# One plain chunk per feed-forward block instead of two, two chunks opened with plain gate blocks, operand sums in another order

## The chip, the cores and the metric

One NeuronCore of one Trainium2 chip runs the whole program. The time is device microseconds (us) from the first to the last instruction of one execution, as the runs report it; lower is better. The engines are named as in the profile: PE (matrix products), PEld (its weight loads), DVE (vector), ACT (scalar/activation), POOL (GpSimd) and SP (the queue that issues most loads from memory).

## What is computed

Two layers of a hybrid encoder over 512 + 256 = 768 tokens of width 1024. Each layer is feed-forward, mixer, feed-forward, with residuals; the first mixer is a gated linear recurrence (HGRN2), the second a windowed attention. The change touches only the four feed-forward blocks:

```python
def swiglu_ffn(x, w1, w2):
    gate, up = jnp.split(x @ w1, 2, axis=-1)
    return (jax.nn.silu(gate) * up) @ w2
...
x = x + 0.5 * swiglu_ffn(rmsnorm(x, norm_g[li, 0]), ffn_w1[li, 0], ffn_w2[li, 0])
```

w1 is 1024 x 5632 (gate columns, then up columns), w2 is 2816 x 1024, everything float32.

## The kernel before

**Products in three passes.** Every float32 operand is split into a high part (`hi`, a cast on ACT) and the rest (`lo`, a subtraction on DVE); a product is hi·hi + hi·lo + lo·hi. So each weight costs an ACT cast and a DVE subtraction before PE can use it: lines 166 and 167 for a plain weight of 128x1024, lines 199 and 200 for the pieces of the scheme below (there one piece in seven, p5, has its subtraction on POOL).

**Chunks and groups.** The 2816 hidden columns are NF = 22 chunks of 128. The first two of a block (PLAIN = 2) are computed plainly: gate and up, two halves of 384 tokens, 8 x 3 products each, 96 matmuls a chunk in all. Every other chunk ("quad", `up_pair`) uses a Winograd-Strassen scheme: the gate tile and the up tile, cut at half the depth, give a11, a12 (gate) and a21, a22 (up), and seven products p1 to p7 of 12 matmuls replace eight, 84 matmuls a chunk. Their order on PE is UP: p1, p7, p2, p5, p4, p6, p3. The p5 and p3 products go into the same PSUM bank `d`; between them, line 446 (`w = w - d`) has to read the bank. After every four chunks a "down" quad multiplies with w2 by the same scheme on 512-wide tiles (order DOWN: p1, p2, p5, p4, p7, p6, p3; 18 matmuls each, 126 in all), and line 506 adds each result to the residual `x`. There are five such groups in a block, so 20 in the program, then two chunks and a plain last product.

**Weights on their way.** `plan_ffn` writes a queue of loads. `load_next` takes its head and issues the loads into raw buffers `wr`: there are four (RAWBUFS), a quad of up chunks takes two (gate tile, up tile), a down quad four, a plain weight one. Two loads that add, both issued by POOL (line 141), form `s3 += a11` (for p7) and `a21 += a22`. Two DVE additions in place (line 206) follow: "second" a11 += a21, and "fourth" a12 += a11; p6 and p3 are split from their results. A raw buffer is free again when its last piece is split: the up tile after p4 and p5, the gate tile after p3.

**What sets the order.** A list scheduler puts each engine's instructions in order; it may move an instruction forward from its place in the program text when its operands and buffers are free. Split weights lie in eight `w` tiles (WBUFS). `held` counts them: a staged piece adds 1 or 2, `release` takes that off again, and `ahead`, called after nearly every product, stages further pieces as long as `held` stays within eight. `take` stages a piece at its use if `ahead` has not done so before. The second and fourth additions are pinned: `keep_in_program_order` makes such an instruction follow the instruction that was written just before it for the same engine. So the place at which a step is written matters for those two, and for the casts that wait for them.

Of the kernel before, what the change touches and what calls it, by code (L numbers as in the profile page):

```python
# [12 lines left out]
AF = mybir.ActivationFunctionType  # L13
# [32 lines left out]


class Trunk:
# [123 lines left out]
    def quad_steps(self, key, raws, srcs, order):  # L172
# [204 lines left out]
    def plan_ffn(self, tag, w1, w2):  # L377
        def up(i):
            gate, up = (w1[:, c * P : (c + 1) * P] for c in (i, NF + i))
            if i < PLAIN:  # L380
                self.plan((tag, i, 0), gate, (NC, P))
                self.plan((tag, i, 1), up, (NC, P))
            else:
                self.plan_quad((tag, i), (gate, up), (NC, P), UP)

        for g in range(GROUPS):
            for i in range(4 * g, 4 * g + 4):
                up(i)
            rows = w2[4 * g * P : (4 * g + 4) * P, :].rearrange("(a k p) c -> k p a c", p=P, k=2)
            srcs = [rows[k][:, :, c * 512 : (c + 1) * 512] for c in range(2) for k in range(2)]  # L390
            self.plan_quad((tag, "down", g), srcs, (2, 512), DOWN)
        for i in range(NF - 2, NF):
            up(i)
        for c in range(2):
            self.plan((tag, "last", c), w2[(NF - 2) * P :, c * 512 : (c + 1) * 512], (2, 512))

    def up_plain(self, tag, j, half):
        pss = []
        for c in range(2):
            wh, wl = self.take((tag, j, c))  # L400
            ps = self.ps(H)
            for k in range(NC):
                b = self.operand(f"b{k // 4}{half}", k % 4)
                self.mm3(ps, (wh[:, k, :], wl[:, k, :]), b, k == 0, k == NC - 1)
                if half == 0 and k in (((), (2, 6)), ((3, 7), (3, 7)))[j][c]:
# [6 lines left out]
        self.nc.vector.tensor_mul(t, t, pss[1])  # L412
        return t

    def product(self, key, name, src, ps, first, last):
        wh, wl = self.take((*key, name))
        for k in range(4):
            a, b = (wh[:, k, :], wl[:, k, :]), self.operand(src, k)
            for i, (x, y) in enumerate(((0, 0), (0, 1), (1, 0))):
                self.nc.tensor.matmul(  # L420
                    ps,
# [3 lines left out]
                    stop=k == 3 and i == 2,  # L425
                    skip_group_check=True,
                )
        self.release((*key, name))

    def up_pair(self, tag, j):  # L430
        nc = self.nc
        key = (tag, j)
        a, b, c, d = (self.ps(H) for _ in range(4))
        v, w, t = (self.tmp(H) for _ in range(3))
        p = lambda name, ps, first, last: self.product(key, name, FACTOR[name], ps, first, last)
        p("p1", a, True, False)
        nc.scalar.copy(v, a)
        self.ahead()
        p("p7", c, True, False)
        nc.scalar.copy(w, c)  # L440
        self.ahead()
        p("p2", a, False, True)
        nc.scalar.activation(a, a, AF.Silu)
        self.ahead()
        p("p5", d, True, False)
        nc.vector.tensor_sub(w, w, d)
        self.ahead()
        p("p4", c, False, True)
        p("p6", b, True, True)
        nc.vector.tensor_sub(v, v, b)  # L450
        nc.vector.tensor_sub(t, c, v)
        nc.vector.tensor_mul(t, t, a)
# [55 lines left out]
    def ffn(self, tag, next_row):  # L508
        for g in range(GROUPS):
            hid = {}  # L510

            def put(name, src, kp):
                if name not in hid:
                    hid[name] = self.big([P, 2, 2, H], F32R)
                self.split(src, hid[name][:, kp, 0, :], hid[name][:, kp, 1, :])

            def gather(ts, kp):
                self.mix(ts[0], ts[1], ts[2], ts[3], lambda name, src: put(name, src, kp))

            if g == 0:  # L520
                ts = {}
                for half in range(2):
                    for j in range(PLAIN):
                        t = ts[2 * j + half] = self.up_plain(tag, j, half)
                        name = f"b{j}{half}"
                        if name != "b01":
                            put(name, t, 0)
                gather(ts, 0)
                self.run_later(len(self.deferred))
            for kp in range(2):  # L530
                if g == 0 and kp == 0:
                    continue
                ts = []
                for j in range(2):
                    for half, t in enumerate(self.up_pair(tag, 4 * g + 2 * kp + j)):
# [753 lines left out]
```

## Time and profile before

| | |
|---|---|
| median of 3 runs | 2816.7 us (2816.09 to 2816.84) |
| the profiled execution: its time | 2815.21 us |
| its span from first to last instruction | 2813.4 us |
| granted PE clock, mean over the span | 0.998 |
| ACT busy | 1324.6 us, 47% of the span |
| POOL busy | 366.5 us, 13% |
| read from memory | 216.39 MB |

The page of the profile is one execution. The row of an engine gives its busy time; in the rows by line, "out<-in xcount | busy, mean ns" are a group of equal instructions, and what stands behind the second bar is how long their engine sat idle before them and what ended that. PE's instructions overlap, so busy time divided by count (not the mean of one) is the pace at which they follow each other.

### The profile page before, as it was taken

The numbers are of one execution on the slowest core, as the hardware profiler recorded it, in microseconds if no ns is written. First come the engines' busy times: TensorE is split into PE (matmuls) and PEld (weight loads), VectorE is DVE, ScalarE is ACT, GpSimd is POOL, SyncE is SP. The second block draws the span as 40 slices with busy tenths as digits, with TensorE's granted clock in tenths as the row PEclk, the third lists the DMA queues.
The fourth block names the chain that finished last, engine by engine and source line by source line (L and its number), as shares of the span: only waits on it lengthen the run. The fifth ranks groups of instructions, "written<-read, shape, count | busy, mean of one in ns | idle before, by whom it ended". The sixth has DMA issues, their size and how long they took to land.

```text
span 2813.4 us, 40558 instructions
## 1 busy us (share of the span) xinstructions
PE 2781.1 (99%) x15225; PEld 2557.6 (91%) x15225; DVE 2162.5 (77%) x3750; ACT 1324.6 (47%) x2453; POOL 366.5 (13%) x402
## 2 busy tenths in 40 slices
PE   8999999999999999999999999999999999999998
PEld 8999999889899889999999999999988789999998
DVE  7788788478577558878878887887858878878877
ACT  7444443434344336444444644444457756444443
POOL 1111121000000001111111111111103211211111
PEclk9999999999999999999999999999999999999999
DMA  6554554311111133555454255545422113655543
GB/s 165 133 126 114 124 142 121 112 46 38 39 45 38 60 97 76 135 131 124 114 127 127 75 136 133 129 112 129 135 72 76 32 52 83 143 135 124 120 114 108
DMA packets 330102, 291.37 MB, mean 104 GB/s; under 512 B 11609, under 2 KB 257841, under 8 KB 329905
## 3 DMA queue, kind: packets, MB, share of 16 engines
q1 hardware_dynamic: 294064, 212.43, 25.8%
q0 software_dynamic: 31680, 62.93, 13.0%
q10 hardware_dynamic: 4160, 13.42, 1.4%
q8 instruction: 119, 1.95, 0.3%
q14 instruction: 79, 0.64, 0.1%
HBM read 216.39 MB, written 9.44 MB: 80 GB/s over the span
## 4 chain that ended last, share of the span: by engine, by line
PE 95%; ACT 2%; DVE 2%; POOL 0%; issue 0%; DMA 0%; DVEq 0%; SPq 0%; ACTq 0%; POOLq 0%
PE ps L420 41%; PE ps L484 20%; PE ps L262 8%; PE ps L261 8%; PE ps L260 8%; PE ps L676 3%; PE ps L770 1%; PE ps L322 1%; PE ps L746 1%; PE ps L1151 1%; ACT big L1129 0%; PE ps L1113 0%; PE ps L1164 0%; PE ps L1114 0%; PE ps L915 0%; PE ps L1163 0%
## 5 line engine op out<-in xcount | busy, mean ns | idle before, releaser
L420 PE MATMUL ps<-big,w 128*128 128x384 f32 x6720 | 1169.2, 334 | 0.0
L420 PEld LDWEIGHTS ps<-big,w 128*128 128x128 f32 x6720 | 1165.9, 188 | 1.6
L199 ACT CAST w<-wr 128x512 fp32r<-128x512 f32 x600 | 416.2, 707 | 684.3 <-PE ps L420 277.6
L484 PE MATMUL ps<-w,big 128*128 128x512 f32 x2520 | 575.3, 389 | 0.0
L484 PEld LDWEIGHTS ps<-w,big 128*128 128x128 f32 x2520 | 472.7, 188 | 97.5
L200 DVE TENSOR_TENSOR w<-wr,w 128x512 fp32r<-128x512 f32 (+1 forms) x520 | 433.5, 837 | 152.8 <-ACT w L199 132.0
L506 DVE SCALAR_TENSOR_TENSOR x<-ps,x 128x512 f32<-128x512 f32 x468 | 301.9, 683 | 10.0 <-PE ps L262 10.0
L141 POOL DMA_DIRECT2D s<-wr x120 | 105.0, 875 | 1536.5 <-DMA wr<-in_ffn_w_dram 632.7
L260 PE MATMUL ps<-w,big 128*128 128x512 f32 x624 | 249.4, 400 | 0.3
L262 PE MATMUL ps<-w,big 128*128 128x512 f32 x624 | 244.7, 392 | 2.1 <-DVE big L989 1.1
L261 PE MATMUL ps<-w,big 128*128 128x512 f32 x624 | 244.0, 391 | 0.0
L260 PE MATMUL ps<-big,w 128*128 128x384 f32 (+2 forms) x640 | 220.8, 346 | 3.4 <-ACT big L265 2.0
L261 PE MATMUL ps<-big,w 128*128 128x384 f32 (+2 forms) x640 | 217.0, 339 | 0.6 <-DVE big L266 0.4
L262 PE MATMUL ps<-big,w 128*128 128x384 f32 (+2 forms) x640 | 215.7, 337 | 0.0
L265 ACT CAST big<-tA 128x384 fp32r<-128x384 f32 x296 | 148.0, 513 | 114.8 <-DVE tA L459 36.2
L167 DVE TENSOR_TENSOR w<-wr,w 128x1024 fp32r<-128x1024 f32 x92 | 111.9, 1222 | 83.6 <-ACT w L166 78.2
L266 DVE TENSOR_TENSOR big<-tA,big 128x384 fp32r<-128x384 f32 x296 | 166.0, 571 | 6.7 <-ACT big L265 4.4
L200 POOL TENSOR_TENSOR w<-wr,w 128x512 fp32r<-128x512 f32 x80 | 131.4, 1643 | 195.5 <-ACT w L199 195.5
L166 ACT CAST w<-wr 128x1024 fp32r<-128x1024 f32 x92 | 96.6, 1052 | 121.5 <-PE ps L261 100.7
L262 PEld LDWEIGHTS ps<-w,big 128*128 128x128 f32 x624 | 117.2, 188 | 28.3 <-DVE big L989 2.0
L141 POOL DMA_DIRECT2D wr<-wr x100 | 87.3, 873 | 403.1 <-DMA wr<-in_ffn_w_dram 165.6
L206 DVE TENSOR_TENSOR wr<-wr,wr 128x512 f32<-128x512 f32 (+1 forms) x120 | 125.3, 1044 | 17.8 <-issue 15.9
(169 smaller groups left out, 3273.6 us busy)
## 6 DMA issues: line engine op xcount, KB each, us to landing
wr<-in_ffn_w_dram SPq DMA_DIRECT2D x264, 512.0 KB, 4.0
s<-in_ffn_w_dram SPq DMA_DIRECT2D x120, 256.0 KB, 3.2
s<-wr POOLq DMA_DIRECT2D x120, 256.0 KB, 4.8
wr<-wr POOLq DMA_DIRECT2D x80, 256.0 KB, 3.8
wr<-in_hg_w_in_dram SPq DMA_DIRECT2D x40, 512.0 KB, 3.8
wr<-wr POOLq DMA_DIRECT2D x20, 512.0 KB, 4.6
spill<-x ACTq DMA_DIRECT2D x12, 512.0 KB, 2.9
x<-spill ACTq DMA_DIRECT2D x12, 512.0 KB, 3.3
```

The lines of the kernel that those rows point to most:

```text
L141: self.nc.gpsimd.dma_start(out, src, accum_op=ALU.add)
L199: nc.scalar.copy(h, src)
L200: (eng or nc.vector).tensor_sub(l, src, h.bitcast(F32))
L206: add = {"second": lambda: nc.vector.tensor_add(a11, a11, a21), "fourth": lambda: nc.vector.tensor_add(a12, a12, a11)}
L260: nc.tensor.matmul(out, a[0], b[0], start=first, stop=False)
L261: nc.tensor.matmul(out, a[0], b[1], start=False, stop=False)
L262: nc.tensor.matmul(out, a[1], b[0], start=False, stop=last)
L265: self.nc.scalar.copy(hi, src)
L266: self.nc.vector.tensor_sub(lo, src, hi.bitcast(F32))
L420: self.nc.tensor.matmul(ps, a[x], b[y], start=first and k == 0 and i == 0, stop=k == 3 and i == 2, skip_group_check=True,)
L484: nc.tensor.matmul(ps, a[x], w[y], start=name == chain and kp == 0 and q == 0, stop=kp == 1 and q == 2, skip_group_check=True,)
L506: self.nc.vector.scalar_tensor_tensor(x, ps, c, x, ALU.mult, ALU.add)
```

## The change

PLAIN becomes 1. Chunks 1 and 2 of a block (OPENED) have their gate computed by `open_pairs` from a plain gate weight, on the first 384 tokens, before the operands of the second half exist; their remaining five products follow as REST: p5, p7, p6, p4, p3. For them the subtraction of p5 goes to DVE. `sums`, which forms the operands t1 to t4 of a block, forms them in the order t1, t3, t2, t4 for both halves of the depth, where it formed all four for one half and then for the other. In `plan_ffn` the plain gate weights of both opened chunks are planned in the branch that every quad chunk takes.

```diff
-PLAIN = 2
+PLAIN = 1
+OPENED = range(PLAIN, PLAIN + 2)
...
+REST = ("p5", "p7", "p6", "p4", "p3")
...
-            split(name, own[name], nc.gpsimd if up and name == "p5" else None)
+            split(name, own[name], nc.gpsimd if order == UP and name == "p5" else None)
...
     def sums(self):
-        for kp in range(2):
-            tiles = (self.tn[(i // 2, i % 2)][:, kp] for i in range(4))
-            self.mix(*tiles, lambda name, src: self.put(name, kp, src))
+        sub = self.nc.vector.tensor_sub
+        quads = [[self.tn[(i // 2, i % 2)][:, kp] for i in range(4)] for kp in range(2)]
+        for kp, (b11, b12, b21, b22) in enumerate(quads):
+            sub(b22, b12, b22)
+            sub(b12, b11, b12)
+            self.put("t1", kp, b12)
+        for kp, (b11, b12, b21, b22) in enumerate(quads):
+            self.put("t3", kp, b22)
+        for kp, (b11, b12, b21, b22) in enumerate(quads):
+            sub(b11, b11, b22)
+            self.put("t2", kp, b11)
+        for kp, (b11, b12, b21, b22) in enumerate(quads):
+            sub(b21, b21, b11)
+            self.put("t4", kp, b21)
...
             else:
-                self.plan_quad((tag, i), (gate, up), (NC, P), UP)
+                for j in OPENED:
+                    self.plan((tag, j, "gate"), w1[:, j * P : (j + 1) * P], (NC, P))
+                self.plan_quad((tag, i), (gate, up), (NC, P), REST if i in OPENED else UP)
...
+    def open_pairs(self, tag, js):
+        opened = {j: (self.ps(H), self.tmp(H)) for j in js}
+        for part in range(2):
+            for j, (a, v) in opened.items():
+                key = (tag, j, "gate")
+                w = tuple(t[:, 4 * part : 4 * part + 4, :] for t in self.take(key))
+                self.multiply(a, w, FACTOR["p2" if part else "p1"], not part)
+                if part:
+                    self.nc.scalar.activation(a, a, AF.Silu)
+                    self.done(key)
+                else:
+                    self.nc.scalar.copy(v, a)
+                self.run_later()
+        return opened
...
-    def up_pair(self, tag, j):
+    def up_pair(self, tag, j, opened=None):
...
+        if opened:
+            p("p5", d, True, False)
+            self.ahead()
+            p("p7", c, True, False)
+            nc.scalar.copy(w, c)
+            nc.vector.tensor_sub(w, w, d)
+            self.ahead()
+            p("p6", b, True, True)
+            p("p4", c, False, True)
+        else:
...
             if g == 0:
-                ts = {}
-                for half in range(2):
-                    for j in range(PLAIN):
-                        t = ts[2 * j + half] = self.up_plain(tag, j, half)
...
+                plain = [self.up_plain(tag, 0, 0)]
+                put("b00", plain[0], 0)
+                opened = self.open_pairs(tag, OPENED)
                 self.run_later(len(self.deferred))
+                plain.append(self.up_plain(tag, 0, 1))
```

Three places show what stands in a row now. The line numbers of the changed kernel are a little higher: 549 is the old 506 (adding to x), 208 the old 206 (second and fourth), 202 the old 200 and 169 the old 167 (subtractions of a split), 489 the old 446, 493 the old 450.

**The queue of loads (SP), second group of the first block.** `wr_257` and `wr_258` are the gate and up tile of one chunk, `wr_260` and `wr_261` of the next, and so on; `s3` is the extra tile for p7. Before:

```order
L151 DMA wr_258_1735<-in_ffn_w1_dram 128x8x128
L151 DMA wr_260_1741<-in_ffn_w1_dram 128x8x128
L151 DMA wr_261_1743<-in_ffn_w1_dram 128x8x128
L185 DMA s3_278_1866<-in_ffn_w1_dram 128x4x128
L151 DMA wr_276_1862<-in_ffn_w1_dram 128x8x128
L151 DMA wr_277_1864<-in_ffn_w1_dram 128x8x128
```

Now:

```order
L153 DMA wr_332_2047<-in_ffn_w1_dram 128x8x128
L153 DMA wr_333_2049<-in_ffn_w1_dram 128x8x128
L153 DMA wr_344_2081<-in_ffn_w1_dram 128x8x128
L153 DMA wr_347_2087<-in_ffn_w1_dram 128x8x128
L187 DMA s3_386_2365<-in_ffn_w1_dram 128x4x128
L153 DMA wr_356_2195<-in_ffn_w1_dram 128x8x128
L153 DMA wr_357_2197<-in_ffn_w1_dram 128x8x128
L153 DMA wr_373_2248<-in_ffn_w1_dram 128x8x128
L153 DMA wr_376_2254<-in_ffn_w1_dram 128x8x128
```

Between the tiles of one chunk (332, 333) and of the next (356, 357) two further loads of the same size stand now (344, 347; then 373, 376): the plain gate weights of chunks 1 and 2 once more.

**The down quad on DVE, second half of it.** `x` rows add a product's results (three rows a product, one for each block of tokens); `wr_331`/`wr_405` is a11 of this down quad. Before, with `ps_359` to `361` holding p7 and the `x_5` to `x_7` rows ahead of it the end of p4:

```order
L506 SCALAR_TENSOR_TENSOR x_7_98<-ps_354_2445,x_7_98 128x512
L206 TENSOR_TENSOR wr_331_2265<-wr_331_2265,wr_333_2269 128x1024
L506 SCALAR_TENSOR_TENSOR x_10_104<-ps_359_2485,x_10_104 128x512
L506 SCALAR_TENSOR_TENSOR x_11_106<-ps_360_2493,x_11_106 128x512
L200 TENSOR_TENSOR w_358_2482<-wr_331_2265,w_357_2481 128x1024
L506 SCALAR_TENSOR_TENSOR x_12_108<-ps_361_2501,x_12_108 128x512
L206 TENSOR_TENSOR wr_332_2267<-wr_332_2267,wr_331_2265 128x1024
```

Now, with p7 in `ps_427` to `429` and p6 in `ps_432` to `434`:

```order
L549 SCALAR_TENSOR_TENSOR x_12_108<-ps_429_2676,x_12_108 128x512
L208 TENSOR_TENSOR wr_405_2504<-wr_405_2504,wr_407_2508 128x1024
L202 TENSOR_TENSOR w_431_2686<-wr_405_2504,w_430_2685 128x1024
L549 SCALAR_TENSOR_TENSOR x_10_104<-ps_432_2689,x_10_104 128x512
L549 SCALAR_TENSOR_TENSOR x_11_106<-ps_433_2697,x_11_106 128x512
L549 SCALAR_TENSOR_TENSOR x_12_108<-ps_434_2705,x_12_108 128x512
L208 TENSOR_TENSOR wr_406_2506<-wr_406_2506,wr_405_2504 128x1024
L202 TENSOR_TENSOR w_436_2715<-wr_406_2506,w_435_2714 128x1024
L169 TENSOR_TENSOR w_450_2759<-wr_437_2718,w_449_2758 128x1024
L169 TENSOR_TENSOR w_453_2765<-wr_438_2720,w_452_2764 128x1024
```

The second addition (208, first row of that line) stood ahead of all three additions of p7's result and stands now behind the last of them; the fourth stands behind the last addition of p6's result, and the split of p3 behind that.

**An up chunk on DVE.** `wr_332` belongs to chunk B, the second of its group, `wr_356` to chunk C, the third; line 489 is B's reading of the bank `d`. Now:

```order
L202 TENSOR_TENSOR w_355_2192<-wr_332_2047,w_355_2192 128x512
L169 TENSOR_TENSOR w_372_2245<-wr_344_2081,w_371_2244 128x1024
L169 TENSOR_TENSOR w_375_2251<-wr_347_2087,w_374_2250 128x1024
L202 TENSOR_TENSOR w_377_2256<-wr_356_2195,w_377_2256 128x512
L202 TENSOR_TENSOR w_378_2272<-s3_358_2199,w_378_2272 128x512
L202 TENSOR_TENSOR w_379_2288<-wr_356_2195,w_379_2288 128x512
L489 TENSOR_TENSOR tA_340_2075<-tA_340_2075,ps_339_2074 128x384
L208 TENSOR_TENSOR wr_356_2195<-wr_356_2195,wr_357_2197 128x512
```

Behind the split of B's p3 stand the splits of two repeated gate weights (169), then C's p1, p7 and p2, and only then B's line 489.

More of the change, by code (lines that the diff above doesn't have):

```diff
@@ L404, in up_plain @@
                 self.mm3(ps, (wh[:, k, :], wl[:, k, :]), b, k == 0, k == NC - 1)
-                if half == 0 and k in (((), (2, 6)), ((3, 7), (3, 7)))[j][c]:
+                if half == 0 and k in ((), (2, 6))[c]:
                     self.run_later()
@@ L413, in up_plain, with product, multiply @@
         return t
-    def product(self, key, name, src, ps, first, last):
-        wh, wl = self.take((*key, name))
+    def product(self, key, name, src, ps, first):
+        self.multiply(ps, self.take((*key, name)), src, first)
+        self.release((*key, name))
+    def multiply(self, ps, w, src, first):
         for k in range(4):
-            a, b = (wh[:, k, :], wl[:, k, :]), self.operand(src, k)
+            a, b = (w[0][:, k, :], w[1][:, k, :]), self.operand(src, k)
             for i, (x, y) in enumerate(((0, 0), (0, 1), (1, 0))):
@@ L431, in up_pair @@
+    def up_pair(self, tag, j, opened=None):
         nc = self.nc
         key = (tag, j)
[L433 to L449, printed above, removed]
+        a, v = opened or (self.ps(H), self.tmp(H))
+        b, c, d = (self.ps(H) for _ in range(3))
+        w, t = (self.tmp(H) for _ in range(2))
+        p = lambda name, ps, first, last: self.product(key, name, FACTOR[name], ps, first)
+        if opened:
[8 more added lines that the diff above has]
+        else:
+            p("p1", a, True, False)
+            nc.scalar.copy(v, a)
+            self.ahead()
+            p("p7", c, True, False)
+            nc.scalar.copy(w, c)
+            self.ahead()
+            p("p2", a, False, True)
+            nc.scalar.activation(a, a, AF.Silu)
+            self.ahead()
+            p("p5", d, True, False)
+            nc.vector.tensor_sub(w, w, d)
+            self.ahead()
+            p("p4", c, False, True)
+            p("p6", b, True, True)
```

14 lines of the change are left out of this document (6 added, 8 removed).

## The prediction

> **What bounds the kernel now.** I read the page first: busy shares, then the chain of work that ended last, then the costliest groups.
>
> ```profile
> span 2813.4 us, 40558 instructions
> ...
> PE 2781.1 (99%) x15225; PEld 2557.6 (91%) x15225; DVE 2162.5 (77%) x3750; ACT 1324.6 (47%) x2453; POOL 366.5 (13%) x402
> ...
> PE 95%; ACT 2%; DVE 2%; POOL 0%; issue 0%; DMA 0%; DVEq 0%; SPq 0%; ACTq 0%; POOLq 0%
> ...
> L420 PE MATMUL ps<-big,w 128*128 128x384 f32 x6720 | 1169.2, 334 | 0.0
> ...
> L484 PE MATMUL ps<-w,big 128*128 128x512 f32 x2520 | 575.3, 389 | 0.0
> ```
>
> PE is busy 99% of the span and carries 95% of the chain: its pace is the time. An up matmul takes 1169.2/6720 = 0.174 us, a down matmul 575.3/2520 = 0.228 us. So a product of an up chunk is 12 x 0.174 = 2.09 us, a chunk 14.6 us, a down quad 28.7 us. The waits of PE, longest first and the last, say how little is left to gain:
>
> ```profile
> PE ps L111 <- DMA tB<-in_hg_g_norm_dram: 7.5, 1, 7.5
> PE ps L915 <- DVE big L266: 3.1, 3, 1.9
> ...
> PE ps L261 <- DVE big L266: 0.4, 1, 0.4
> ```
>
> There are eleven such rows, 23 us together, none at an up or down product. A change can gain only by giving PE fewer instructions; it can lose wherever it uncovers a wait. The cover, in one down quad and the four chunks behind it:
>
> ```profile
> 257.50:286.00 28.50, 28.50 (x127) 23.59 (x126) 28.09 (x46) 10.19 (x17) 4.92 (x5) 1.00 0.58 136
> 286.00:344.50 58.50, 58.50 (x338) 58.46 (x338) 41.62 (x69) 27.54 (x49) 10.08 (x10) 1.00 0.51 123
> ```
>
> Columns after the length: PE, PEld, DVE, ACT, POOL busy, PE clock, share of the transfer engines, GB/s. DVE has almost no slack in a down quad and 17 us in four chunks.
>
> **The change part by part.** *Removed:* one plain chunk a block. 96 matmuls become 84, 48 fewer over four blocks: 48 x 0.174 = 8.4 us off PE, the whole of the possible gain.
>
> *Added:* the planning line stands in the branch of every quad chunk. So both plain gate weights are queued ahead of each of 21 quads: 42 a block, 168 in all, where 8 are used. What the 160 repeats cost, by a plain weight's split:
>
> ```profile
> L167 DVE TENSOR_TENSOR w<-wr,w 128x1024 fp32r<-128x1024 f32 x92 | 111.9, 1222 | 83.6 <-ACT w L166 78.2 <-PE ps L420 4.7
> ...
> L166 ACT CAST w<-wr 128x1024 fp32r<-128x1024 f32 x92 | 96.6, 1052 | 121.5 <-PE ps L261 100.7 <-PE ps L420 20.1 <-DVE w L167 0.3
> ...
> q1 hardware_dynamic: 294064, 212.43, 25.8%
> ...
> wr<-in_ffn_w_dram SPq DMA_DIRECT2D x264, 512.0 KB, 4.0
> ...
> s<-wr POOLq DMA_DIRECT2D x120, 256.0 KB, 4.8
> wr<-wr POOLq DMA_DIRECT2D x80, 256.0 KB, 3.8
> wr<-wr POOLq DMA_DIRECT2D x20, 512.0 KB, 4.6
> ```
>
> ACT gets 168 us more and DVE 196, spread over the span; four chunks bring DVE eight repeats, 9.8 us, to 51.4 of 58.5 us. The 84 MB more are 102 us of transfer time (3.4 us a MB by q1's row). All that fits beside PE: no engine becomes the bound by its sum, and I cost it at nothing. Two other things are not free. The repeats hold two of the four raw buffers, so a chunk's tiles load only when the chunk before has left its own. And `held` grows by 4 with every quad and is never taken down (a repeat overwrites its staged entry, and is released once at most). After the third quad it stays at eight or more, `ahead` returns at once, and each piece is staged where it is used. Casts and splits still move forward; the pinned additions don't. So now the walk, with one group's order.
>
> *Pinned additions (40 places).* In the profile the second and fourth additions and their splits stand far ahead of use:
>
> ```profile
> 257.45 28.76 PE L484 MATMUL ps<-w,big 128*128 128x512 f32 x126
> ...
> 269.28 1.22 DVE L206 TENSOR_TENSOR wr<-wr,wr 128x1024 f32<-128x1024 f32 x1
> ...
> 271.67 1.23 DVE L200 TENSOR_TENSOR w<-wr,w 128x1024 fp32r<-128x1024 f32 x1
> ...
> 276.24 1.23 DVE L200 TENSOR_TENSOR w<-wr,w 128x1024 fp32r<-128x1024 f32 x1 [0.41 <-ACT w L199]
> ...
> 270.58 1.06 ACT L199 CAST w<-wr 128x1024 fp32r<-128x1024 f32 x1 [4.61 <-DVE wr L206]
> ...
> L506 DVE SCALAR_TENSOR_TENSOR x<-ps,x 128x512 f32<-128x512 f32 x468 | 301.9, 683 | 10.0 <-PE ps L262 10.0
> ```
>
> p6 starts 5 x 4.1 us after 257.45, at 278.0; its split ends at 272.9. Now, after p7's last matmul: addition to x 0.68, second addition 1.22, cast 1.06, and PE may start p6; three matmuls (0.68) run with the high part while the subtraction takes 1.23. Idle: 0.68 + 1.22 + 1.06 + (1.23 - 0.68) = 3.5, and 0.3 for five hand-overs (the cast above starts 0.08 after its addition): 3.8 us. p3 waits likewise behind p6. Two places, 20 quads: 40 x 3.8 = **152 us**. Bounds 140 (no hand-overs) and 200 (DVE still has queued work ahead).
>
> *First chunk after a down quad (20).* The small pieces cost:
>
> ```profile
> L199 ACT CAST w<-wr 128x512 fp32r<-128x512 f32 x480 | 291.6, 620 | 413.3 <-PE ps L420 212.3 <-PE ps L484 64.7 <-DVE wr L206 57.3
> ...
> L200 DVE TENSOR_TENSOR w<-s,w 128x512 fp32r<-128x512 f32 x120 | 82.5, 687 | 17.4 <-ACT w L199 17.1
> ...
> L450 DVE TENSOR_TENSOR tA<-tA,ps 128x384 f32<-128x384 f32 x80 | 44.1, 551 | 41.5 <-PE ps L420 41.2
> ...
> 285.78 1.88 DVE L506 SCALAR_TENSOR_TENSOR x<-ps,x 128x512 f32<-128x512 f32 x3
> ```
>
> DVE instructions that follow each other overlap a little: three of 0.68 take 1.88, a pace of 0.60. Let p6 end at 0. The addition to x and the fourth addition end at 2.0 and free the raw buffer of the next gate tile, whose load lands 4.0 later with its issue, at 6.2. Meanwhile the cast and split of p3 end at 4.4; PE, which has three matmuls of p3 behind it, needs 15 x 0.228 = 3.4 more and comes to the new chunk at 7.8. On DVE two repeats (to 6.8) and two additions to x (8.0) stand ahead of its p1 split, which ends at 8.6; PE has two matmuls of high parts to do (0.35) and then waits 0.45. p1 ends at 10.3. The s3 transfer, issued at 6.2, lands at 11.0; cast and split end at 12.4, where PE could have gone on at 10.65: 1.75 lost. **20 x 2.2 = 44 us**; 0 if loads land earlier, 80 if each stands behind one repeat (512 KB, 1.8 us by q1's row).
>
> *Inside a group (20).* PE adds p3(B) into bank `d` only when B's line 489 has read it, and line 489 stands behind C's p7 split. On the same clock A ends on PE at 24.7, and p3(B) is due six products later, at 37.2. The split of p3(A) ends at 16 (its cast stands behind the copy that waits for p7(A), 14.4) and frees the buffer for B's up tile. That lands at 20.0 and is added into by 24.5, with issue; B's p7 and p2 splits, the second addition and line 493 bring the split of p4(B) to 27.2. This frees the buffer for C's gate tile: landed 31.2, s3 36.0, cast and split 37.3, p2 37.9, line 489 38.4. **20 x 1.2 = 24 us**; 0 to 60, since one transfer that is 2 us late comes through in full. C and D have line 489 ahead of the next p7 and just make it.
>
> *Into the down quad (20).* D starts at 55.1 by the same walk; its p3 split, behind C's last vector steps and two repeats, ends at 61.3. The fourth raw tile of the down quad loads only then (65.4) and is added into the third (70.0); cast and split of the down quad's p5 end near 72.4, and D's last six steps (0.47 to 0.60 apart), which stand behind that split, bring b10's low part near 76.4. PE, done with D at 69.8, wants it for p2 at 69.8 + 4.1 + 1.1 = 75.0. **20 x 1.5 = 30 us**; 0 to 70.
>
> *A block's start (4).* Chunks 1 and 2 give PE 60 matmuls, 10.4 us, but the loop of their up tile (4.0 + 3.8, then two additions and splits of p4, p6, p3 at 0.6 to 0.7 with casts between) is about 14: 2 x 3.6 = 7; **28 us**, 0 to 60. The new order of `sums` and the p5 subtraction on DVE lie under the plain second half (48 matmuls, 8.4 us): t1 needs six steps of 0.95 at most, 5.7 us; bare, that would cost 23 in all. Mixers: their casts carry no pin and stand where they stood; 0.
>
> ```profile
> L266 DVE TENSOR_TENSOR big<-big,big 128x768 fp32r<-128x768 f32 x64 | 58.2, 952 | 11.5 <-ACT big L265 11.5
> ```
>
> *The clock.* One pause of PE inside the program shows it:
>
> ```profile
> 26.00:28.00 2.00, 0.72 (x4) 0.33 (x3) 1.58 (x4) 1.99 (x4) 0.54 (x1) 1.00 0.58 101
> 576.00:578.00 2.00, 0.96 (x6) 0.96 (x7) 0.98 (x2) 0.98 (x1) 0.00 (x0) 1.00 0.00 0
> 578.00:580.00 2.00, 2.00 (x11) 2.00 (x10) 1.08 (x4) 0.30 (x1) 0.00 (x0) 0.50 0.00 0
> 580.00:582.00 2.00, 2.00 (x14) 2.00 (x13) 1.53 (x3) 0.61 (x1) 0.00 (x0) 0.64 0.00 0
> ...
> 577.04 2.58 PE L676 MATMUL ps<-big,big 128*128 128x128 f32 x12 [1.74 <-ACT big L701]
> ```
>
> After 1.74 us without work the granted clock was 0.5 for two microseconds and 0.64 for the next two, some 3.4 us in all; a pause of 1.28 at 26 to 28 did nothing. The pauses at p6 and p3 are near 3.2 us in one piece, so I let each cost 3.4 us of half clock, less what falls into the pause: 1.5. **40 x 1.5 = 60 us**; 0 to 100.
>
> The Trainium skill, "TensorE: Matmul & The Clock Gate", Part 1, sets the fall of the clock at a whole idle window of about 3.4 us. By that rule our pauses would mostly leave the clock alone and the sum would lose its last term; the trace's fall after 1.74 us speaks against it.
>
> **Sum.** On the profiled execution's 2815.2 (1.5 below the median): 2815.2 - 8.4 + 152 + 44 + 24 + 30 + 28 + 60 = 3144.8; on the median's footing 3146 us. All low ends give 2948, all high ends 3378.
>
> **The rivals.** *The clock stays up:* 3146 - 60 = 3086. For it: a pause like ours has no row in this trace, and 1.28 us left the clock alone. Against: 1.74 us did not. In the Trainium skill, the rule of "TensorE: Matmul & The Clock Gate" quoted above would lead here. *The load loop sets the pace of the up chunks:* if load, add and splits take 17 us a chunk instead of about 15, each of 80 chunks lasts 2.4 longer, 192 us in place of the 54 for group and down quad: 3284. For it: two buffers for a chunk, transfers at 0.51 share before the repeats; against: after the first chunk each piece from p2 on is split some 5 us or more ahead of PE in the walk (p3(C) near 46, due at 53), and the 28.7 us of a down quad let the loads catch up. *Only the pins cost:* loads land in time and the clock holds, 2815.2 - 8.4 + 152 + 1.5 = 2960. *Faster, as the text of the change suggests:* the waits stay covered and the 48 matmuls are saved, 2808. That would need less than 0.2 us lost at each of the 40 pinned places, and their shortest chain has four operations of 0.68 to 1.23 us in a row with PE empty; only an order on the chip other than the built one could do that.
>
> **How the numbers follow.** Forecast 0.56, clock stays 0.19, load loop 0.12, only pins 0.10, faster 0.03. 0.2% (about 6 us) is what a measurement here can tell from no change; all cases but the last lie far above it: slower 0.96, same 0.01, faster 0.03. The range 3020 to 3290 takes in the forecast, the clock's rival and the load loop, and leaves out 0.13 besides tails.
>
> **What would show it.** Right: about 160 more plain splits (DVE's busy time up by some 195 us, ACT's by 170); waits of PE at the down line for ACT casts and DVE splits, 40 each, over 100 us together; PE idle over 300 us; a clock of 0.5 behind such pauses and a mean under 0.99. Wrong: PE still 99% busy, down quads of 28.7 us, the additions of line 208 ahead of p7's results. A wait at up products for DVE far above 100 us would say that the load loop rules.

## The result, and the profile after

Median 3553.3 us (3538.9 to 3556.4, five runs) against 2816.7 (2816.1 to 2817.3, five runs): ratio 1.260, 95% interval 1.2585 to 1.2611. Slower, as forecast, but 407 us beyond the forecast of 3146 and outside its range. The page of the profiled execution (3540.0 us):

```profile
PE 3038.3 (86%) x15177; PEld 2708.4 (77%) x15177; DVE 2383.7 (67%) x3954; ACT 1466.4 (41%) x2633; POOL 363.8 (10%) x406
...
L438 PE MATMUL ps<-big,w 128*128 128x384 f32 x7056 | 1393.2, 359 | 310.5 <-ACT tA L480 186.9
...
L527 PE MATMUL ps<-w,big 128*128 128x512 f32 x2520 | 676.9, 429 | 159.6 <-ACT w L201 123.4
...
wr<-wr POOLq DMA_DIRECT2D x84, 256.0 KB, 6.2
```

Its waits of PE, the longest first (total, times, longest), and from the list of cores its span and the granted clock:

```profile
PE ps L438 <- ACT tA L480: 186.9, 52, 6.9
PE ps L527 <- ACT w L201: 123.4, 40, 3.4
PE ps L438 <- ACT w L201: 103.1, 44, 5.3
PE ps L527 <- DVE x L549: 28.9, 19, 3.3
```

```profile
core 0: 3538.2 us, clock 0.927
```

PE has 48 matmuls fewer (15177 for 15225) and is busy 257 us longer, because its clock was halved for part of the time: (1 - 0.927) x 3538 = 258 us lost, against 0.002 x 2813 = 6 before. It also waits 310.5 us at the up products (line 438) and 159.6 at the down products (527), where it waited for nothing before. The balance: 2815.2 - 8.4 + 310.5 + 159.6 + 252 = 3529, 11 us short of the profiled time.

One group, from the first matmul of a down quad to that of the next (start, length, and in brackets the idle time before the row):

```profile
347.64 4.28 PE L527 MATMUL ps<-w,big 128*128 128x512 f32 x18
353.46 16.60 PE L527 MATMUL ps<-w,big 128*128 128x512 f32 x72 [1.54 <-DVE x L549]
373.11 6.00 PE L527 MATMUL ps<-w,big 128*128 128x512 f32 x18 [3.04 <-ACT w L201]
382.15 0.98 PE L527 MATMUL ps<-w,big 128*128 128x512 f32 x3 [3.04 <-ACT w L201]
383.48 5.25 PE L527 MATMUL ps<-w,big 128*128 128x512 f32 x15 [0.35 <-DVE w L202]
388.57 2.39 PE L438 MATMUL ps<-big,w 128*128 128x384 f32 x12
394.08 16.25 PE L438 MATMUL ps<-big,w 128*128 128x384 f32 x84 [3.12 <-ACT w L201]
410.63 2.74 PE L438 MATMUL ps<-big,w 128*128 128x384 f32 x12 [0.30 <-ACT w L201]
417.04 16.58 PE L438 MATMUL ps<-big,w 128*128 128x384 f32 x84 [3.67 <-ACT tA L480]
436.27 14.84 PE L438 MATMUL ps<-big,w 128*128 128x384 f32 x84 [2.65 <-ACT tA L480]
456.61 13.11 PE L438 MATMUL ps<-big,w 128*128 128x384 f32 x60 [5.50 <-ACT tA L480]
469.56 4.28 PE L527 MATMUL ps<-w,big 128*128 128x512 f32 x18
```

The group takes 121.9 us; with no wait uncovered it takes 86.9 (rows of the first experiment, below). Of the 35 us more, 8.0 are waits inside the down quad, 15.2 waits in the four chunks, the remaining 11.8 mostly the clock (0.92 in the mean over this group): where 18 down matmuls take 4.28 us at full pace, the 18 behind the first 3.04 take 6.00. The forecast had 3.4 us a group for the chunks.

What the chunks wait for, in the timeline of the same stretch (p3 of chunk A is split at the end of the first row, p3 of B at the end of the second, p3 of C in the fifth, p3 of D in the last):

```profile
398.18 1.46 DVE L202 TENSOR_TENSOR w<-wr,w 128x512 fp32r<-128x512 f32 x2
...
417.53 1.28 DVE L202 TENSOR_TENSOR w<-wr,w 128x512 fp32r<-128x512 f32 x2
...
424.00 0.86 POOL L143 DMA_DIRECT2D wr<-wr  x1 [4.39 <-DMA wr<-in_ffn_w_dram]
...
429.37 0.69 DVE L208 TENSOR_TENSOR wr<-wr,wr 128x512 f32<-128x512 f32 x1 [2.34 <-DMA wr<-wr]
...
435.22 0.68 DVE L202 TENSOR_TENSOR w<-wr,w 128x512 fp32r<-128x512 f32 x1
...
435.76 0.46 ACT L480 COPY tA<-ps 128x384 f32<-128x384 f32 x1
...
435.92 5.23 SPq L153 DMA_DIRECT2D wr<-in_ffn_w_dram  x3
...
456.75 0.68 DVE L202 TENSOR_TENSOR w<-wr,w 128x512 fp32r<-128x512 f32 x1
```

The split of p3(B) ends at 418.8 and frees a load buffer. C's up tile is loaded into it, and POOL issues the adding transfer at 424.0 (5.2 us); it has landed by 429.2 (5.2), and the second addition, the fourth and three splits bring the split of p3(C) to 435.9 (6.7); the next load leaves at 435.92. That loop is 17.1 us, where a chunk on PE is 14.6. It is the shortest of this group: from p3(A) (399.6) to p3(B) it takes 19.2, from p3(C) to p3(D) (457.4) 21.5, and the mean over the 48 loops of the 16 groups that follow another group of their block is 19.3. PE's chunks follow each other at that pace. The page's adding transfer into `wr` took 6.2 us at the median, before 3.8. Line 480's copy, for which PE waits, stands on ACT behind this loop's casts.

### The profile page after: what moved, and what is told of

Read it like the earlier page. It is cut to its first block, busy times and chain, and to the rows that moved or that the text cites. A ratio compares the mean times of both kernels' runs of the same rounds, so it can differ in the third digit from the quotient of the medians.

```text
span 3538.2 us, 41318 instructions
## 1 busy us (share of the span) xinstructions
PE 3038.3 (86%) x15177; PEld 2708.4 (77%) x15177; DVE 2383.7 (67%) x3954; ACT 1466.4 (41%) x2633; POOL 363.8 (10%) x406
## 3 DMA queue, kind: packets, MB, share of 16 engines
q1 hardware_dynamic: 470896, 301.57, 29.5%
## 5 line engine op out<-in xcount | busy, mean ns | idle before, releaser
L438 PE MATMUL ps<-big,w 128*128 128x384 f32 x7056 | 1393.2, 359 | 310.5 <-ACT tA L480 186.9
L438 PEld LDWEIGHTS ps<-big,w 128*128 128x128 f32 x7056 | 1340.4, 205 | 361.0 <-ACT tA L480 203.5
L527 PE MATMUL ps<-w,big 128*128 128x512 f32 x2520 | 676.9, 429 | 159.6 <-ACT w L201 123.4
L201 ACT CAST w<-wr 128x512 fp32r<-128x512 f32 (+1 forms) x608 | 412.4, 703 | 903.6 <-DVE wr L208 531.0
L527 PEld LDWEIGHTS ps<-w,big 128*128 128x128 f32 x2520 | 515.3, 209 | 316.0 <-ACT w L201 140.4
L202 DVE TENSOR_TENSOR w<-wr,w 128x512 fp32r<-128x512 f32 (+1 forms) x532 | 461.2, 872 | 219.2 <-ACT w L201 186.9
L169 DVE TENSOR_TENSOR w<-wr,w 128x1024 fp32r<-128x1024 f32 x252 | 305.9, 1223 | 97.5 <-ACT w L168 81.9
L168 ACT CAST w<-wr 128x1024 fp32r<-128x1024 f32 x252 | 262.2, 1049 | 126.3 <-PE ps L263 99.8
L262 PE MATMUL ps<-w,big 128*128 128x512 f32 x624 | 248.9, 399 | 0.3
L264 PE MATMUL ps<-w,big 128*128 128x512 f32 x624 | 244.6, 392 | 0.0
L263 PE MATMUL ps<-w,big 128*128 128x512 f32 x624 | 244.0, 391 | 0.0
L202 DVE TENSOR_TENSOR w<-s,w 128x512 fp32r<-128x512 f32 x124 | 84.9, 688 | 231.4 <-ACT w L201 224.3
L201 ACT CAST w<-s 128x512 fp32r<-128x512 f32 x124 | 74.7, 618 | 335.0 <-DMA s<-wr 290.9
L262 PE MATMUL ps<-big,w 128*128 128x256 f32 (+2 forms) x512 | 177.7, 348 | 2.0 <-ACT big L267 2.0
L263 PE MATMUL ps<-big,w 128*128 128x256 f32 (+2 forms) x512 | 174.0, 340 | 0.7 <-DVE big L268 0.5
L264 PE MATMUL ps<-big,w 128*128 128x256 f32 (+2 forms) x512 | 172.7, 337 | 0.0
```

The lines of the kernel that those rows point to most:

```text
L168: self.nc.scalar.copy(hi, raw)
L169: self.nc.vector.tensor_sub(lo, raw, hi.bitcast(F32))
L201: nc.scalar.copy(h, src)
L202: (eng or nc.vector).tensor_sub(l, src, h.bitcast(F32))
L262: nc.tensor.matmul(out, a[0], b[0], start=first, stop=False)
L263: nc.tensor.matmul(out, a[0], b[1], start=False, stop=False)
```

## The experiments

Three things could make this loss: the count `held`, which rises by 4 a quad so that every piece is split only at its use; the splits of the 160 repeated blocks; and their loads, with the load buffers they occupy.

### The blocks planned once

```diff
-                for j in OPENED:
-                    self.plan((tag, j, "gate"), ...)
+                if i == PLAIN:
+                    for j in OPENED:
+                        self.plan((tag, j, "gate"), ...)
```

> The gate blocks of chunks 1 and 2 are planned once per feed-forward block (8 loads in the program instead of 168); all else of the change stays: one plain chunk, two chunks opened ahead, operand sums in the new order. Theory A (the 160 repeated loads and the count of held buffers that they let grow are the whole loss): 2800 to 2830 us, the waits at the up products and the down products back to what they were, mean clock above 0.99. Rival (opening two chunks costs by itself, because their first products and copies crowd the start of a block): more than 2850 us, with the idle time at the four block starts and not at the down products.

Measured: 2846.7 us, ratio 1.011 (1.0097 to 1.0127). Its waits of PE at up and down products, and one group:

```profile
PE ps L439 <- ACT tA L474: 11.9, 4, 3.7
PE ps L528 <- DVE x L550: 8.2, 4, 2.4
...
PE ps L439 <- DVE w L202: 5.9, 4, 4.4
```

```profile
302.35 58.43 PE L439 MATMUL ps<-big,w 128*128 128x384 f32 x336
360.62 28.76 PE L528 MATMUL ps<-w,big 128*128 128x512 f32 x126
389.21 58.43 PE L439 MATMUL ps<-big,w 128*128 128x384 f32 x336
```

The time lies between the two ranges. The repeats, with the count that they raise, are 707 of the 737 us. A group is back at 389.21 - 302.35 = 86.9 us. What stays is four waits of each kind, one in the first group of each block: 30 us more than before, and with the 8.4 of PE's saving 38 (the forecast's term was 28).

### The count alone, and the repeats without it

The count alone: planned once, and at the first step of each later up quad

```diff
+            if up and name == order[0] and key[1] > PLAIN:
+                self.held += 4
```

> The gate blocks are planned once, so no repeated load and no repeated split; but the count of held weight buffers is raised by 4 at each later up quad, as it rises in the change, so that every block is split only when its product is due. Theory A (the load loop needs the repeats; last-moment splitting makes only the waits at p6 and p3 of the 20 down quads, some 130 us, about 90 us of slowed clock behind them, some 30 us into the down quads and a few at block starts): 3000 to 3100 us, up chunks at 14.6 to 15.5 us. Rival B (last-moment splitting is the whole loss): 3450 to 3560 us, up chunks at 19 to 20 us.

The repeats without the rising count: a repeat gets a key of its own, is loaded and split, and its two buffers are taken off the count at once.

```diff
+            if key[-1] == "again":
+                self.held -= 2
+                return
```

> All 160 repeated gate blocks are still loaded and split, but the count of held weight buffers is corrected after each, so that blocks are again split ahead of their use. Theory A (the up chunks run at the pace of a loop through the four load buffers, of which the repeats hold two): only the waits at p6 and p3 of the down quads go, about 130 us and about 90 us of slowed clock that follows them, so 3250 to 3400 us, and the up chunks still take 18 to 20 us each. Rival B (splitting at the last moment is the whole loss, the loads and their buffers cost nothing): 2820 to 2900 us, the chunks at about 14.6 us.

Measured: 3094.6 us (ratio 1.099, 1.0976 to 1.1013) and 3199.7 us (1.136, 1.1345 to 1.1379). So the count costs 248 us over the kernel that plans once, and the repeats 353; together they cost 707, 106 more than their sum. In the first the waits are where the forecast had put them:

```profile
PE ps L530 <- ACT w L201: 122.8, 40, 3.3
PE ps L530 <- DVE x L552: 9.3, 4, 3.2
```

In the second the 40 waits are gone, the chunks are slow without them, and there are new waits at the down products, which no expectation had:

```profile
PE ps L531 <- DVE x L553: 70.4, 26, 4.5
```

```profile
449.63 19.92 PE L442 MATMUL ps<-big,w 128*128 128x384 f32 x108
472.07 10.14 PE L442 MATMUL ps<-big,w 128*128 128x384 f32 x48 [2.51 <-ACT tA L484]
483.55 14.88 PE L442 MATMUL ps<-big,w 128*128 128x384 f32 x84 [1.34 <-DVE tA L493]
502.18 18.48 PE L442 MATMUL ps<-big,w 128*128 128x384 f32 x96 [3.75 <-DVE tA L493]
520.50 27.40 PE L531 MATMUL ps<-w,big 128*128 128x512 f32 x120
```

Four chunks take 520.50 - 449.63 = 70.9 us for 58.4. Each of the two effects works alone. Theory A was right for the count; for the repeats it was right that the chunks stay slow, but they take 17.7 us here and not 18 to 20, its range began 50 us too high, and it had no wait left at the down products.

### What of a repeat costs: load, split, or the buffer in between

With the rising count as in the change, the repeats were loaded and not split:

```diff
+            if key[-1] == "again":
+                return
```

> The 160 repeated gate blocks are loaded into their buffers but never split (no ScalarE cast, no VectorE difference for them); the count of held buffers still rises. Theory A (the repeats cost by holding two of four load buffers and by their transfers): the repeats' buffers come free as soon as their turn in the order comes, so the loop loses only the 2 splits that stand in it; 3350 to 3550 us, chunks at 18 to 19.5 us. Rival C (the extra splits, 170 us on ScalarE and 195 us on VectorE in the order ahead of the products, are the loss): 3000 to 3200 us, close to what the last-moment splitting costs without any repeat.

Measured: 3116.9 us (ratio 1.107, 1.1053 to 1.1086), 22 over the count alone. Theory A's number fell: the loads, 84 MB, cost next to nothing when nobody waits to read them. But this did not yet say that the splits' work is the loss, since a block that nobody reads gives its buffer back as soon as it has landed. So one kernel kept the buffer taken without the work, and one did the work without a buffer:

```diff
+            if key[-1] == "again":
+                r, s = self.stat(1), self.stat(1)
+                self.nc.scalar.copy(r, raw[:, 0, :1])
+                self.nc.vector.tensor_sub(s, raw[:, 0, :1], r)
+                return
```

> As the run in which the 160 repeated gate blocks were loaded and not split (3116.9 us), but at the place of each split ScalarE and VectorE now read one column of the block, so its load buffer stays taken until the same place in their order as in the change; no weight buffer is written and nearly no work added. Theory H (the split costs by keeping two of four load buffers taken until it is done, so that the next loads on SP's queue wait): 3450 to 3560 us, nearly all of the change. Rival W (it costs by its own work, a cast of 1.05 us and a difference of 1.2 us for each block in the order ahead of the products, and by the weight buffers it fills): 3110 to 3180 us.

```diff
-            self.nc.scalar.copy(hi, raw)
-            self.nc.vector.tensor_sub(lo, raw, hi.bitcast(F32))
+            src = self.ident.unsqueeze(1).to_broadcast([P, NC, P]) if key[-1] == "again" else raw
+            self.nc.scalar.copy(hi, src)
+            self.nc.vector.tensor_sub(lo, src, hi.bitcast(F32))
...
+                        self.queue.append((key, (), (NC, P), None))
```

> The counterpart: the 160 repeats are not loaded, but their splits are made all the same, from a constant tile into weight buffers (ScalarE cast, VectorE difference, two weight buffers each), with the count of held buffers rising as in the change. Theory H (held load buffers): 3110 to 3200 us, as there is nothing to hold. Rival W (the work of the splits): 3450 to 3560 us.

Measured: held and not split 3272.3 us (1.162, 1.158 to 1.1658); split and not loaded 3156.9 (1.121, 1.1193 to 1.1226). Over the count alone that is 178 and 62; both together, the change itself, are 459. So the work is not the loss by itself, but the buffer alone gives only two fifths of it: neither of the two ranges for the held kernel was right. In the kernel that splits and does not load, the loss stands in the down quad, at its second product:

```profile
PE ps L532 <- DVE x L554: 58.4, 20, 4.6
```

The count alone has 9.3 us there. The next run left all splits and took the repeats out of the quads' four buffers:

```diff
-            t = self.wp.tile([P, 1024], F32, tag="wr", name=self.name("wr"), bufs=RAWBUFS)
+            again = key[-1] == "again"
+            tag, bufs = ("wg", 1) if again else ("wr", RAWBUFS)
+            t = self.wp.tile([P, 1024], F32, tag=tag, name=self.name(tag), bufs=bufs)
...
-SLOTS = 21
+SLOTS = 20
```

> The full change with the repeats' loads taken out of the four load buffers: of each pair of repeated gate blocks only the first is loaded, into one buffer of its own, and both splits are made from it; the count of held buffers rises as in the change, and the quads have all four load buffers again (one working tile fewer, 20 instead of 21). All splits are there, and 80 of 160 loads. If the pace of the up chunks in the change comes from the two load buffers that the repeats hold, with the split's work in the loop: 3140 to 3200 us, as in the run that split without loading (3156.9 us), with the adding transfer back near 3.7 us. If the loads' bytes beside the splits' work make it, whatever the buffers: 3300 to 3450 us.

Measured: 3118.3 us (1.107, 1.1056 to 1.1087), 22 below the first range. One group of it:

```profile
395.19 4.28 PE L542 MATMUL ps<-w,big 128*128 128x512 f32 x18
399.91 17.04 PE L542 MATMUL ps<-w,big 128*128 128x512 f32 x72 [0.44 <-DVE x L564]
420.00 6.17 PE L542 MATMUL ps<-w,big 128*128 128x512 f32 x18 [3.05 <-ACT w L207]
429.22 0.97 PE L542 MATMUL ps<-w,big 128*128 128x512 f32 x3 [3.05 <-ACT w L207]
430.55 5.31 PE L542 MATMUL ps<-w,big 128*128 128x512 f32 x15 [0.35 <-DVE w L208]
435.70 58.41 PE L453 MATMUL ps<-big,w 128*128 128x384 f32 x336
493.94 4.28 PE L542 MATMUL ps<-w,big 128*128 128x512 f32 x18
```

With the same 160 splits the four chunks take 58.4 us again, without one wait, and the down quad keeps its two waits of 3.05. Besides the buffers, half of the loads fell away, and loads alone were worth 22; whether all 160 loads beside the splits would cost more was not run. The adding transfer fell only to 5.2 us at the median; a slow transfer costs nothing where the loop has four buffers.

In the mean over the same 16 groups the stretch of the four chunks, from the last matmul of one down quad to the first of the next, takes 79.7 us in the change, 66.8 with the buffer held and no split, 58.2 with the repeats in a buffer of their own, 58.1 with splits and no loads and 57.6 with the count alone; the down quad takes 42.0, 41.2, 42.3, 44.0 and 41.4. So what the shared buffers cost stands in the chunks, and what the splits cost without them in the down quad.

The same two parts with the count corrected (the buffer of their own gave no result with that correction, so it is measured with the rising count only):

> All 160 repeated splits are made, from a constant tile and without a load, and the count of held weight buffers is corrected after each. If the load buffers are what costs: 2840 to 2880 us, 170 us of casts and 195 us of differences hidden beside the products. If the splits' work costs by itself: 3000 us or more, near the run with repeated loads and splits (3199.7 us).

> All 160 repeated blocks are loaded into the four load buffers, none is split, and the count of held weight buffers is corrected after each. Nothing reads these blocks, so their buffers come free as soon as they have landed. If loads cost only through the buffers that a waiting split keeps taken: 2845 to 2880 us. If the order of the buffers (each quad gets the same two again) or the bytes cost by themselves: 2950 to 3200 us.

Measured: all splits without loads 2856.6 us (1.0142, 1.0125 to 1.0159), all loads without splits 2861.6 (1.016, 1.0145 to 1.0175), each inside its first range. The whole set, medians in us:

| repeated blocks | count corrected | count rising |
|---|---|---|
| none | 2846.7 | 3094.6 |
| split, not loaded | 2856.6 | 3156.9 |
| loaded, not split | 2861.6 | 3116.9 |
| loaded, one column read | | 3272.3 |
| half of them loaded, into their own buffer, all split | | 3118.3 |
| loaded into the four buffers and split | 3199.7 | 3553.3 |

In either column loading or splitting alone costs 10 to 62 us, both through the shared buffers 353 and 459.

### The clock, and line 480's copy

The count alone, with 13 more matmuls ahead of p6 and of p3 in each down quad, into banks that nothing reads:

```diff
+                if i == 0 and name in ("p6", "p3"):
+                    idle = ps if name == "p6" else self.ps()
+                    for _ in range(FILL):  # FILL = 13
+                        self.nc.tensor.matmul(idle, a[0], w[0], start=True, stop=True)
```

> The run with last-moment splitting and no repeat (3094.6 us, mean clock 0.957, so about 133 us lost to the clock) with 13 matmuls more, into banks that nothing reads, ahead of p6 and of p3 in every down quad, where TensorE waited 122.8 us in 40 places; 13 such matmuls take 3.0 us at the full clock, so they fill the pauses and do not end much later. If the pauses of 3 us themselves pull the clock down for a window: mean clock above 0.985 and 2970 to 3010 us, a hundred us less with 520 matmuls more. Rival (the clock does not fall for these pauses but for others): 3090 to 3120 us, the clock still about 0.957.

Measured: 3018.6 us (1.072, 1.0704 to 1.0736), 76 us less with 520 matmuls more; the clock rose from 0.957 to 0.991:

```profile
core 0: 3017.7 us, clock 0.991
```

```profile
PE ps L535 <- ACT w L202: 17.6, 21, 1.2
```

Shown: the pauses themselves pull the clock down. The time is 9 us above the expected range and the gain 24 short of the hundred expected; 17.6 us of waiting stay, the rest of the shortfall was not followed.

The copy of line 480 on DVE, in the full change:

```diff
-            nc.scalar.copy(v, a)
+            nc.vector.tensor_copy(v, a)
```

> The full change, but the copy out of bank a after p1 of an up chunk (line 480) is made by VectorE instead of ScalarE. Theory A (that copy is late because it stands on ScalarE behind casts of the next chunk's blocks, which wait for the transfer that adds into them): the 187 us of waiting at line 480's copy go or move to a VectorE row; since the loop through the load buffers has its own pace, the gain is at most a third of them: 3480 to 3560 us. Rival B (ScalarE's order is itself what sets the pace of 19 to 20 us per chunk): 3350 to 3430 us, chunks of 17 us or less.

Measured: 3545.7 us (1.259, 1.2575 to 1.2613), no difference from the change that can be told. Most of the wait changed its name:

```profile
PE ps L438 <- DVE tA L480: 144.0, 37, 5.5
...
PE ps L438 <- ACT big L267: 63.8, 16, 5.2
```

The longest row of PE's waits in the change named the last link, not the cause.

### The parts that were meant

From the kernel that plans once: the sums in the old order; then no opened chunk (`OPENED = range(0)`) with the new order of sums; then that with the old order.

> The gate blocks planned once (2846.7 us), with the operand sums of a block's start back in the old order, so of the change only the one plain chunk and the two opened chunks remain. If the new order of sums does its part, the products of the opened chunks wait longer: 2855 to 2880 us. If it does nothing, or delays the splits of the first quad on VectorE: 2835 to 2847 us.

> One plain chunk and the new order of sums, but no chunk opened ahead and so no gate block planned at all, once or again: all other chunks are plain quads. TensorE then reaches the first quad after half the cover that two plain chunks gave the sums. If opening earns what it costs: 2860 to 2900 us, with waits for the sums at the four block starts of 10 to 20 us each. If the opened chunks are themselves what costs 30 us in the kernel that plans them once: 2805 to 2835 us.

> One plain chunk, no opened chunk, the operand sums in the old order: the one part of the change that takes 48 matmuls away and nothing else. If the new order of sums serves the first quad where nothing is opened: slower than the same with the new order (2833.1 us), by 5 to 20 us. If the new order is what delays the weight splits there: 2808 to 2825 us, which could beat the kernel before.

Measured: 2850.2 us (1.0118, 1.0104 to 1.0132), 2833.1 (1.0051, 1.0038 to 1.0065) and 2826.2 (1.0034, 1.0022 to 1.0046). The first lies between its two ranges, the second inside its second, the third 1 us above its second. With opened chunks the order of sums makes no difference that can be told (2846.7 and 2850.2); without them the new order is some 7 us slower. Opening costs 14 to 24 us. No part of the change beats the kernel before, though each of these has 48 matmuls fewer; what holds the last one 10 us above it was not followed further.

## Why the prediction was wrong

**The step that failed** is the one that set the rival of the load loop aside: "after the first chunk each piece from p2 on is split some 5 us or more ahead of PE in the walk (p3(C) near 46, due at 53), and the 28.7 us of a down quad let the loads catch up". The walk gave the loop 15 us a chunk, with the load at 4.0 and the addition at 4.5 us, durations of a program in which two loads leave at a time. With the repeats' loads leaving beside them and their buffers held, both took 5.2 in the loop shown, and the loops 17.1 to 21.5 in its group, 19.3 in the mean. So PE waits in each chunk anew: 3.67, 2.65, 5.50 in the group shown. In place of the terms 44 + 24 = 68 us stand 435 (3553.3 less the 3118.3 of the same splits with a buffer of their own and half the repeated loads), clock included; by the groups it is 20 x (79.7 - 58.2) = 430.

**The rival named the cause and priced it too low.** It had a loop of 17 us and 3284 us. One of the three loops of the group shown takes that long; the mean is 19.3, and PE's chunks follow each other 436.27 - 417.04 = 19.2 and 456.61 - 436.27 = 20.3 us apart. Its own sign, waits at the up products far above 100 us, came, but for ACT (186.9 and 103.1) and not for DVE. Why the repeats' splits add 281 us to the 178 of a held buffer stays open; nearly all of it stands in the chunks (79.7 against 66.8 us a group). DVE's time for the two differences, 1.22 us each, does not explain it: in the loop shown they end at 421.3, and DVE, after C's p1, stands idle for 3.4 us before it can split C's p7.

**Pins:** 152 forecast; 123.4 + 6.9 = 130 measured, in 40 places, under the lower bound of 140. Mechanism and place right, as the count alone shows; the size was 17% too high.

**Into the down quad:** 30 forecast, 28.9 measured, at the place that was named. The agreement is luck: the forecast had a late load of the down quad's fourth raw tile, but the wait stays at 27.4 us with a buffer of the repeats' own and grows to 58.4 with no repeated load at all. It comes with the splits' work.

**A block's start:** 28 forecast, 38 measured; 14 to 24 of it is the opening, as the last experiments show, and the rest also stands without an opened chunk.

**The work of the repeats:** costed at nothing. That holds with the count corrected (10 us), but with the count rising, as in the change, the splits alone cost 62. The 102 us of transfer time in the prediction is a slip: 84 MB at its own 3.4 us a MB are 286, and q1's row grew by about 318 (29.5% of 3538 us against 25.8% of 2813).

**The clock:** 60 forecast, 252 measured. Two errors: a pause at p6 can cost 2.9 us (worked out at the end), not 1.5, and it was counted at the 40 pinned places only, while the pauses of the load loop set it off too. Read in half-microsecond windows, the change has 111 stretches below full clock, 512 us together.

Against the count alone the other terms look right by luck: pins, into the down quad and their clock, 152 + 30 + 60 = 242, stand against 248, where the waits are 122.8 and 9.3 and the clock takes some 110 ((1 - 0.957) x 3090 = 133, less the 23 of the kernel that plans once), so errors cancel.

The Trainium skill, "Perfetto Trace Analysis", section Optimization Strategy, says that the same gap repeating on the engine that should be saturated can mean too few buffers for the next tile. The change's trace agrees: a gap of 2.65 to 5.50 us in each late chunk, gone where the repeats have a buffer of their own.

## What to carry to other kernels

Here a load that nobody needs cost little by its bytes alone and little by its work alone (10 to 62 us); it cost most by the buffer it kept until its turn came. When something new goes into a shared ring of load buffers, write down the loop from the freeing of a buffer to the next freeing, with durations for as many transfers as will then leave together, and compare it with the time of one round on the bound engine: above that, every round pays, and the longest row of waits can name an innocent copy at the end of it. Follow several rounds in a row: the three of the group shown differ by 4 us. And a counter that gates prefetching needs a test that it comes back to its start.

## What the runs showed of the hardware

A pause of 3.05 us is long enough to halve PE's clock. In the kernel with the count alone the 46 stretches of half clock all begin on one grid of 3.41 us. Four windows on that grid, around one pause at p6 (the clock stands third from the end, PE's busy time first):

```profile
407.31:410.73 3.42, 1.37 (x7) 0.79 (x5) 2.51 (x3) 0.10 (x1) 0.00 (x0) 1.00 0.00 0
410.73:414.14 3.41, 2.41 (x6) 1.79 (x7) 1.23 (x1) 0.94 (x1) 0.00 (x0) 0.50 0.54 159
414.14:417.55 3.41, 3.41 (x10) 2.64 (x9) 0.69 (x1) 0.00 (x0) 0.86 (x1) 0.50 0.38 67
417.55:420.97 3.42, 1.27 (x6) 0.70 (x4) 2.52 (x3) 0.20 (x1) 0.00 (x0) 1.00 0.06 10
```

and the row of the matmuls behind that pause:

```profile
411.73 7.09 PE L530 MATMUL ps<-w,big 128*128 128x512 f32 x18 [3.04 <-ACT w L201]
```

PE was busy for 1.37 us of the first window, and the next is at half clock; in that one the pause still takes 1.0 us, and the third is at half clock too, to 417.55. That is 6.8 us, of which PE works from 411.73 and so loses 5.8/2 = 2.9. Where a pause falls on the grid decides: another of 3.05 us, from 116.71 to 119.75, halved the clock only at 120.60, after its end, and for one window. Counted over this trace, with the ends of matmuls as the profile models them: of the windows at full clock in which PE idled for less than 40%, 765, none was followed by half clock; of those over 60%, 33, every one; between, 25, it went either way. Over the program the stretches lasted one window or two: 13 and 32, and one at the very end. The Trainium skill, "TensorE: Matmul & The Clock Gate", Part 1, has a window of about 3.4 us, and a fall after a whole window without work. The lengths agree with that window; the fall does not, as 60% of a window without work was enough.
